# A new hand-written order for a grouped attention kernel, and VectorE's own addition of its terms in one more head

## The chip, the cores and the metric

The kernel runs on one core of one Trainium2 chip. The core has TensorE (matrix multiplication, called PE in the profile, its weight loads PEld), VectorE (DVE), ScalarE (ACT), GpSimd (POOL) and SyncE (SP), which work side by side and meet at semaphores. The metric is the device time of one execution in microseconds (us). Three timed executions and one profiled execution are at hand.

## The reference

```python
batch, n_q_heads, n_kv_heads, seq, head_dim = (8, 8, 2, 1024, 64)
scale = 1.0 / np.sqrt(head_dim)
for g in range(n_kv_heads):                      # four query heads share one k and v
    scores = scale * np.matmul(q_group, k_group.transpose(0, 1, 3, 2))
    scores_max = np.max(scores, axis=-1, keepdims=True)
    attn = np.exp(scores - scores_max)
    attn = attn / (np.sum(attn, axis=-1, keepdims=True) + 1e-08)
    output[:, q_start:q_end, :, :] = np.matmul(attn, v_group)
```

All arrays are float32. There are 64 attention problems (8 batches by 8 query heads), each 1024 by 1024 with 64 dimensions.

## The kernel before, in words

**The unit of work.** The 64 problems are called heads here and are numbered 0 to 63. The scores of a head are made transposed, keys on the partitions, in eight chunks. A chunk is made by two matmuls (line 791), each of 128 keys by 512 queries, one on the upper and one on the lower 64 rows of the array; they fill one of three PSUM slots, `sp0` to `sp2`, of 128 x 1024 float32 values. There are 512 chunks in all, here also called scores and counted from 0. A slot can be filled again only when the engine that reads it is done, so three chunks at most are on their way.

**Two engines take the exponential.** Of the 512 chunks, 377 go to ScalarE, which applies its exponential and writes the tile `pt` (line 801). The other 135 go to VectorE, which builds the exponential from the bits of a 16-bit number: `dpass` (line 813) reads PSUM and writes `yt`; then, for two chunks together where it can, `zh` (line 822) takes the mantissa into `zt`, `two` (line 830) takes the exponent into `et`, and `mul` (line 840) multiplies `zt` by `yt`. The exponential is the sum `et + zt`. In most heads nobody adds them: TensorE multiplies both with v and sums in PSUM, which costs it a second set of matmuls for such a chunk. In the last `TAIL` heads VectorE adds them itself (`add`, line 846), and TensorE has one set.

**GpSimd helps.** The planner hands some columns of a `mul` to GpSimd (line 775) wherever a free stretch of the shared work allows, but not in the last five heads (`GTO = 5`). GpSimd also issues the loads of q, k and v that change the type to bfloat16 (lines 560 and 550).

**The product with v.** For each of eight pieces of 128 queries in a head, eight matmuls (line 859) of 128 x 128 weights against 65 columns of `va` (v and a column of ones, which gives the row sums) are accumulated, plus one for each second term. The head before the last is stored through the same banks `ops0` and `ops1`, seven pieces at a time: `rec` (line 924) takes the reciprocals of the sums, `norm` (line 934) multiplies into `ost`, and SyncE stores a head when it is complete (line 943). The last head is accumulated chunk by chunk in a score slot (line 899) as its chunks come in. q and k are transposed on TensorE (line 569) and copied out by VectorE (lines 577 and 584).

**What sets the order.** Nothing is scheduled by the compiler. A long text, `ORDER`, is read letter by letter by the class `Plan`, which keeps one clock for each engine with costs in nanoseconds (the `M_` constants). For TensorE a letter is a score for ScalarE (`A`), a score for VectorE of the current head or of one of the next (`a`, `b`, `c`, `d`), three matmuls with v (`V`), a transposition (`T`), a warming matmul (`F`), a step of the first or last head (`E`, `L`), or a wait (`W`). For VectorE it is a `dpass` (`p`, `P`), a step of the chain in place 0, 1 or 2 of the list of open chains (digits), an eviction (`t`), `rec` (`r`, `R`), `norm` (`n`) or a wait (`i`). Which engine reads the next letter depends on whose clock is behind. The constants emit no instruction: they decide which engine a letter belongs to, how wide a part of a `mul` GpSimd is given, and when a load is due. The result is one list of instructions for each engine, in a fixed order. `W` and `i` leave nothing in the program; an engine waits where its next instruction's data or buffer isn't ready.

Of the kernel before, what the change touches and what calls it, by code (L numbers as in the profile page):

```python
# [18 lines left out]
M_SEE = 51  # L19
M_PAIR = 226  # L20
M_PTAIL = 205
M_SWITCH = 99
M_MM = 30.3
M_PVTAIL = 180
M_ACT = 917
M_ATAIL = 107
# [23 lines left out]
PB = 7  # L50
NPIECE = 8
GRAIN = 3
TAIL = 3
CHN = 2
LONG = 6
GFROM = 2
# [5 lines left out]


ORDER = """
ATAtWWWWWWWWWWWWWWWWWWWTAtFWEAbEpAEWWWWWaApEWEAFWW0WWWWbAEpWWAEWW0WWWTAtFFWW0WWWAbFFWWWWApEWWWWAR0cW
WWWAPWWWWWWWWWWWWAWWnWWWTRnVA0VVtVVVVA0WbWWWApVVVVVVVVVA0cWWWApVVVVVVVVA0WbWWWWApVVVVVVARWnWcVVVpVAV
VVA0WA0VVVT0VVtVVVVARnWbWVApVVVVVVA0VT0AVtVVVVA0cWWWApVVVVVVVVARnbWWWApVVVVVVVVA1cWWWApVVVVVVVVA00bW
WWWApVVVVVVVAR1bVVVPAVVVVVAnAV1VT0VVVVtVVARWWnWaAVpVVVVVVVAWW0WWWbApVVVVVVVVA0WbWWApVVVVVVVVVVARnAVT
1VVVVtVVVVA0WbWWApVVVVVVVVA0Vb0WAVpVVVVVVVVVAWRWW1WbAVPVVVVVVVVAWWnWWWbA0VVVVpVVVVVAVVV0VVVAAR1VTnVV
VVtVVAW1WWWbWApVVVVVVVVA0WbWWiWiWiWiWiAipVVVVVVVVAR1bWWWWAPVVVVVVVVAnbWW0WWAVpVVVVVVVA0WWWcWAVpVVVVV  # L70
VVARW0WAWVVT0VVVVtAVnVVVA0bWWWWWApVVVVVVVA1AVV0TVVVtVVVVA0bWWARPVVVVVVVVAnbViVipAVVVVA0WAR0VVVTnVVVt
VVVA0WWaWWApVVVVVVVVA0bVVpAVVVVVA0aVVApVVVVVVARnbVVpVAVVVVA1AVVTRnVVVVtVVA0WWWaWA0VVpVVVVVVVAW0WWWbA
VpVVVVVVVVARW1WbWWAVPVVVVVVVVAWnWWWbWA0VpVVVVVVVVVA0AVT1VVVtVVVVA1bWWWWARPVVVVVVVVAnWaVipVAVVVVA01Wb
VVVpVAVVVVVA0bWWWARVPVVVVVVVAnWWAWa1VVVVVpVVVAVVV0VVAAR0VTnVVVVtVVA0WWaWApVVVVVVVVA0WT0AVtVVVVARnaWW
WWApVVVVVVVVA0WaWWApVVVVVVVVVVVA0W0aWAVpVVVVVVVVVVVA0bWARVPVVVVVVVVVVAnAV1TVV0VVVVVtVAV0VVaARPVVVVVV
AVVnVaAipVVVVVAVVV1VAa1VVVVVpAVVVVVAR0naWWWApVVVVVVVVA1AVT0VVVVtVVVA0WaWWApVVVVVVVVARnaWWWWApVVVVVVV
VA0a0WWWAVpVVVVVVVVA0WWaWApVVVVVVVVVVARnbWWWApVVVVVVVAV0T0VAtVVVV0VaARVPVVAVVVVVnVAA0VVT0VVVtVVVA0aV
VpVAVVVVVARnaWWWApVVVVVVVVA0b0WWWAVpVVVVVVVAW0WWWaAVpVVVVVVVARWnWaWWApVVVVVVVVA0A0WWWaV0VVVVVpVVAVVV
VVRA0AVTnVVVtVVVA0WaVVpAVVVVVARnAVT0VVVVtVVA0WWWaWApVVVVVVVVA0aWWWApVVVVVVVVARnaWWWAVpVVVVVVVA1WWaWW
AVpVVVVVVVA0WWbWWApVVVVVVVVVARW0nWAVT1VVVVtVVVVA0AWWWa0VVVVVVVpVVVAVVVVA0aVRVPVVAVVVanAVpVVVAVVV0VVA  # L80
0bVApVVVVVVArnAVVT1VVtVVVVA0aWWWWApVVVVVVVVA0a0WWWAVpVVVVVVVARW1WaWWAVPVVVVVVVAnWWaWWA0VVpVVVVVVAVRV
1VAAnVVVT0VVtVVVVA0WaVVApVVVVVA0WWaWWWApVVVVVVVVAR1aWWWAPVVVVVVVVAnaWW0WAVpVVVVVVVVA1WbWAVpVVVVVVVVV
A0aWARVnVVVVVVpVVAVVVVVVRVAnT01AVtVVVVVV0AAV0TVVVtVVVVVA0aWWAipVVVVVVVVVaRnAWWWApVVVVVVVVVV0Ab0WWWWA
pVVVVVVVVARWnWaWWAVpVVVVVVVA0WWbWApVVVVVVAV0V0bAVpVVVVVVAV1VVARAnVVVT0VVVtVVVVVA0bWAVpVVVVVVVVARnAVV
T0VVtVVVA0WWaWWAVpVVVVVVVA0WWbWWAVpVVVVVVVA0WaWWARVPVVVVVVVAnVVVV1VAb0WWWApVVVVVVVVAR0WbWWWAVPVVVVVV
VAnWT1AVtVVVVA1bWWWWAipVVVVVVVVARnbWWWApVVVVVVVVA00AVT0VVVVtVVVARW0WbWWAVPVVVVVVVVAnbVipAVVVVVVV0Ab0
WWAVpVVVVVVVVAR0WbWWAVPVVVVVVAVnT1VAVtVVVVA1bWWARPVVVVVVVVAnbV0ipVAVVVVVV1AcV0VAVVVpVAVVVVVAR0bVVPAV
VVVVAnAV0VVT0VVVtVAV0VbARVPVVVVVVVAnWbWWAipVVVVVVVVVA0c0WWAVpVVVVVVVVARWW0WaWAVPVVVVVVVVAnWAWT1VVVtV
VVA1bVARPVVVVVVVAnbWWWA0pVVVVVVVVA1bWWWApVVVVVVVVAR1cWWWAPVVVVVVVVAnWAV0T1VVVtVVVA1WbWWWApVVVVVVVVV0
AcWAVRPVVVVVVVVVAnT1AVtVVVA1WbVVpAVVVVVVVRA0ncWWApVVVVVVVA1WAVVT1VVVtVVVVAR0bWWAVPVVVVVVVVVVAnWWcWAi  # L90
pVVVVVVVVVVA0AV0VVVVVVRV0bAVPVVVVVVVVAncWAipVVVVVVVVVV0AAR0VTnVVVVVtVAWW0WWWWbAVpVVVVVVA0WWWcWAVpVVV
VVVVARWW0WAVTnVVVtVVVA0WbWApVVVVVVVVA0WcWWWWWApVVVVVVVAR0AVVVnVVVVV0VbAipVVVVVAV0VVAcVpVVVVVAVVRVV0A
A0VVVVVnVVA0WbVVVVVVVVRAPVVVVVAnWWcWApVVVVVVVVA0A0VT0VVtVVVVVARnbWAVpVVVVVVVVA0AVVV0VVVVVV0VAbVVVpAV
VVVVA0VAAVVrVnVVVVVVVVVVRAnAVx0VVVV0VVV0VVVVVV0AAVVVVVVVRVnVVVAAVVVVVVVVVaApVVVVVVVVVVVranAApVVVVVVV
VVV0VVVa0AAVpVVVVVVVVVxVVRV0VVAAAVnVVVVVV0VVVVVVVVVVVVVVV0VVVVRV0VVVLnLLR0VVVVVVVVnVVVVVV0VVVVLLRnLL
LFFRFn
"""


# [29 lines left out]
class Plan:  # L129
# [121 lines left out]
    def dve(self, s):  # L251
# [26 lines left out]
        elif what in "pP":  # L278
            _, sl, j, c = s.dq.pop(0)
            n = len(STEPS) if j >= nj - TAIL else 3  # L280
            if s.open and s.open.nsteps != n:
# [74 lines left out]
    def turn(self, s, mode):  # L356
        if s.mode != mode:
            s.tP += M_SWITCH
            s.waste += M_SWITCH
            s.mode = mode  # L360

    def pe(self, s):
# [4 lines left out]
        if kind in "Aabcd":  # L367
# [12 lines left out]
            else:  # L380
                s.dcount[j] += 1
                if j == 0:
                    s.twice.append(c)
                if j < nj - TAIL:
                    s.mms[j] += 1
        elif kind == "V":
# [5 lines left out]
            s.ev.append((s.tP, "pv", s.pc, s.done, n))  # L392
            s.tP += n * M_MM
            s.done += n
# [9 lines left out]
        elif kind == "E":  # L404
# [5 lines left out]
            s.ev.append((s.tP, "pvf", c, s.fleft, None))  # L410
            s.tP += NPIECE * M_MM * (1 + (c in s.twice))
            if not s.fleft:
# [5 lines left out]
        elif kind == "L":  # L418
# [8 lines left out]
            s.ev.append((s.tP, "pvl", c, s.left, None))  # L427
            s.tP += NPIECE * M_MM
            if not s.left:
# [38 lines left out]
def kernel(  # L468
# [261 lines left out]
    def terms(j, par, only=range(NC)):  # L730

        for ci in only:
            c = ci if par == 0 else (ci + NH) % NC
            if (j, c) in where:
                ch, i = where[(j, c)]
                if j < NJ - TAIL:
                    yield ci, et[ch].bitcast(BF16)[:, i, par, :]
# [240 lines left out]
```

## Time and profile before

| what | us |
|---|---|
| median of three runs | 370.01 (369.92 to 370.11) |
| profiled execution, its own time | 369.21 |
| span of the profiled execution, first to last instruction | 367.3 |
| TensorE busy | 358.4 |
| VectorE busy | 353.4 |
| ScalarE busy | 353.3 |
| GpSimd busy | 258.5 |

The profiled execution is 0.80 us below the median of the timed runs, and 1.9 us of its time lie outside the span. A matmul counts as busy from its issue to its modelled end, and the next one starts long before that; a TensorE instruction that waits for a slot behind others does not show as idle. So the share of TensorE is read from the chain of waits and from the distance of its instructions, not from its busy time. VectorE instructions overlap as well: the next one begins some 0.08 us before the end of the one before it, where it does not depend on it.

### The profile page before, as it was taken

The page shows a single profiled execution, that of the slowest core. Times are in us where ns is not written, and L with a number is a line of the kernel's source. Part 1 is how long each engine was busy: PE and PEld are TensorE (multiplying, and loading weights), DVE is VectorE, ACT ScalarE, POOL GpSimd, SP SyncE. Part 2 cuts the span into 40 slices and gives each one's busy share as a digit, 9 for nine tenths or more (in the row PEclk, how much of TensorE's full clock was granted, in tenths as well). Part 3 has the DMA queues.
Part 4 walks back from the last instruction along what each step waited for, and adds up shares of the span by engine and source line. Part 5 has one row for each costly group of instructions (what it writes and reads, how often), then busy time and mean ns, then how long its engine had stood idle before and what let it go on. Part 6 is the DMA issues. An engine that isn't in the chain of part 4 may idle for free.

```text
span 367.3 us, 14608 instructions
## 1 busy us (share of the span) xinstructions
PE 358.4 (98%) x6498; PEld 239.0 (65%) x6498; DVE 353.4 (96%) x547; ACT 353.3 (96%) x381; POOL 258.5 (70%) x286
## 2 busy tenths in 40 slices
PE   8899999999999999999999999999999999999995
PEld 4466666666666765666666676766666667667675
DVE  4999999999999999999999999999999999999886
ACT  6999999999999999999999999999999999999981
POOL 5278878886899799894979878777787887520000
PEclk9999999999999999999999999999999999999999
DMA  7565156363257335255254426354353554112013
GB/s 146 101 113 113 62 104 117 48 141 82 68 102 112 106 89 102 59 110 129 72 100 87 104 75 141 66 98 109 90 86 85 129 116 75 60 46 89 32 59 145
DMA packets 39119, 34.62 MB, mean 94 GB/s; under 512 B 18192, under 2 KB 30608, under 8 KB 38928
## 3 DMA queue, kind: packets, MB, share of 16 engines
q0 software_dynamic: 10880, 12.19, 24.0%
q1 hardware_dynamic: 27888, 21.11, 18.5%
q8 instruction: 50, 0.82, 0.9%
q10 hardware_dynamic: 288, 0.39, 0.3%
q14 instruction: 13, 0.11, 0.1%
HBM read 27.13 MB, written 18.74 MB: 125 GB/s over the span
## 4 chain that ended last, share of the span: by engine, by line
PE 50%; DVE 41%; ACT 5%; issue 2%; DMA 1%; POOL 0%; DVEq 0%; POOLq 0%
PE ops L859 26%; PE sp L791 21%; DVE yt L813 20%; DVE et L830 5%; ACT pt L801 5%; DVE zt L822 5%; DVE ost L934 4%; DVE zt L840 3%; PE sp L569 3%; DVE qt L577 2%; DMA qs<-in_q_dram 1%; DVE rec L924 1%; DVE kt L584 1%; PE sp L899 1%; PE ops L879 0%
## 5 line engine op out<-in xcount | busy, mean ns | idle before, releaser
L801 ACT ACTIVATE pt<-sp 128x1024 bf16<-128x1024 f32 x377 | 350.8, 1033 | 2.9 <-PE sp L791 2.0
L775 POOL TENSOR_TENSOR zt<-yt,zt 128x560 bf16<-128x560 bf16 (+15 forms) x176 | 217.1, 1245 | 50.0 <-DVE zt L822 33.0
L859 PE MATMUL ops<-va,pt 128*128 128x65 bf16 x2904 | 179.4, 194 | 0.0
L791 PE MATMUL sp<-qt,kt 64*128 64x512 bf16 x1024 | 169.3, 382 | 3.2 <-ACT pt L801 0.9
L813 DVE TENSOR_SCALAR yt<-sp 128x1024 uint16<-128x1024 f32 x135 | 163.7, 1213 | 3.0 <-PE sp L791 2.5
L859 PEld LDWEIGHTS <-pt 128*128 128x128 bf16 x2904 | 138.6, 97 | 30.3 <-issue 30.3
L859 PE MATMUL ops<-va,zt 128*128 128x65 bf16 x1064 | 137.2, 194 | 0.0
L859 PE MATMUL ops<-va,et 128*128 128x65 bf16 x1024 | 131.7, 194 | 0.0
L859 PEld LDWEIGHTS <-et 128*128 128x128 bf16 x1024 | 87.1, 98 | 19.7 <-issue 19.7
L859 PEld LDWEIGHTS <-zt 128*128 128x128 bf16 x1064 | 90.9, 97 | 7.7 <-issue 7.7
L791 PEld LDWEIGHTS <-kt 64*128 64x128 bf16 x1024 | 49.7, 93 | 57.8 <-issue 33.6
L822 DVE TENSOR_SCALAR zt<-yt 128x2048 uint16<-128x2048 uint16 (+1 forms) x69 | 47.5, 688 | 0.6
L830 DVE TENSOR_SCALAR et<-yt 128x2048 uint16<-128x2048 uint16 (+1 forms) x69 | 47.1, 683 | 0.0
L934 DVE TENSOR_TENSOR ost<-ops,rec 128x448 f32<-128x448 f32 (+2 forms) x73 | 44.6, 611 | 1.1
L840 DVE TENSOR_TENSOR zt<-yt,zt 128x1144 bf16<-128x1144 bf16 (+36 forms) x63 | 38.3, 608 | 0.0
L560 POOL DMA_DIRECT2D qs<-in_q_dram x32 | 24.4, 763 | 9.4 <-PE sp L569 7.6
L577 DVE COPY qt<-sp 128x1024 bf16<-128x1024 bf16 (+1 forms) x32 | 21.5, 673 | 0.8 <-PE sp L569 0.8
L569 PE MATMUL sp<-ident,qs 128*128 128x128 bf16 x252 | 19.3, 219 | 0.3 <-DMA qs<-in_q_dram 0.2
L569 PEld LDWEIGHTS <-qs 128*128 128x128 bf16 x252 | 14.6, 98 | 1.6 <-issue 1.1
L924 DVE RECIPROCAL rec<-ops 128x7 f32<-128x7 f32 (+2 forms) x73 | 14.1, 193 | 0.9 <-PE ops L859 0.9
L770 POOL MEMSET tick<- 128x1 bf16 x55 | 11.4, 207 | 0.0
L560 POOL DMA_DIRECT2D ks<-in_k_dram x8 | 5.9, 737 | 5.9 <-PE sp L569 5.9
(44 smaller groups left out, 51.4 us busy)
## 6 DMA issues: line engine op xcount, KB each, us to landing
out_dram<-ost SPq DMA_DIRECT2D x63, 256.0 KB, 2.1
qs<-in_q_dram POOLq DMA_DIRECT2D x31, 256.0 KB, 4.2
kt<-kt SPq DMA_DIRECT2D x30, 64.0 KB, 2.5
va<-vd SPq DMA_DIRECT2D x30, 64.0 KB, 3.4
ks<-in_k_dram POOLq DMA_DIRECT2D x7, 256.0 KB, 4.5
vd<-in_v_dram POOLq DMA_DIRECT2D x7, 256.0 KB, 4.4
q<-in_q_dram ACTq DMA_DIRECT2D x1, 256.0 KB, 3.2
vs<-in_v_dram SPq DMA_DIRECT2D x1, 256.0 KB, 4.1
```

What stands on the lines that cost most here:

```text
L560: return nc.gpsimd.dma_start(out=t[:, 0:n, :], in_=x[lo : lo + n].rearrange("h (p s) d -> p h (s d)", p=128))
L569: nc.tensor.transpose(view[:, 0, c * 128 : (c + 1) * 128], src[:, c, :], ident)
L577: ins = nc.vector.tensor_copy(out=t[:, 0:n, :], in_=src)
L775: begun[j] = gps = nc.gpsimd.tensor_tensor(out=z, in0=flat(yt[j])[:, lo : lo + w], in1=z, op=ALU.mult)
L791: now = nc.tensor.matmul(sps[x][:, half, :], lhsT=t[lo : lo + D, c // NH, ci % NH * 128 : (ci % NH + 1) * 128], rhs=qt[j][lo : lo + D, 0, ...
L801: exps.append(nc.scalar.activation(out=p, in_=where_s[(j, c)], func=AF.Exp, scale=scale))
L813: vec = nc.vector.tensor_scalar(out=yt[ch][:, i, :, :], in0=where_s[c], scalar1=EXP_A, scalar2=EXP_B, op0=ALU.mult, op1=ALU.add,)
L822: vec = nc.vector.tensor_scalar(out=zt[j][:, 0:c], in0=yt[j][:, 0:c], scalar1=0x7F, scalar2=0x3F00, op0=ALU.bitwise_and, op1=ALU.bitwise_or,)
L830: vec = ins = nc.vector.tensor_scalar(out=et[j][:, 0:c], in0=yt[j][:, 0:c], scalar1=0x7F80, scalar2=None, op0=ALU.bitwise_and,)
L840: vec = nc.vector.tensor_tensor(out=z, in0=flat(yt[j])[:, 0 : cols[0]], in1=z, op=ALU.mult)
L859: ended[job] = nc.tensor.matmul(ops[plan.group_of[x] % 2][:, lo : lo + D + 1], lhsT=p[:, qs * 128 : (qs + 1) * 128], rhs=va[(b * G + h // ...
L934: vec = nc.vector.tensor_tensor(out=to, in0=src, in1=by, op=ALU.mult)
```

## The change

Two costs in the plan, the number of heads in which VectorE adds its terms, and the whole text `ORDER` are replaced. No function changes.

```diff
-M_SWITCH = 99
-M_MM = 30.3
+M_SWITCH = 96
+M_MM = 30.9
...
-TAIL = 3
+TAIL = 4
...
 ORDER = """
-ATAtWWWWWWWWWWWWWWWWWWWTAtFWEAbEpAEWWWWWaApEWEAFWW0WWWWbAEpWWAEWW0WWWTAtFFWW0WWWAbFFWWWWApEWWWWAR0cW
...
-LFFRFn
+ATAtWWWWWWWWWWWWWWWWWWWWTAtFFEAbEpEAWWWWWWAWWWWWWWWWWWaEpWWWEAFWWWWW0WWbAEpWAEFWW0WWTAtFFWW0WWWWAbF
...
+VVVRV0LLLLLnLLRLnVVVVVRVVnVVVVVVVVVVVVWWWWWWWWWWWWWWWWWWWWWWWWWWWWWWRWWWWWWWWWWWWWWWWWWWWWWWn
 """
```

`M_SWITCH` is what the plan charges TensorE for going from scores to other matmuls or back, and `M_MM` what it charges for one matmul with v. In what the two programs issue, the following differs; everything that is not named has the same number of instructions and the same sizes.

| engine | instructions | before | after |
|---|---|---|---|
| TensorE | matmuls with v | 5128 | 5120 |
| TensorE | changes between scores and other matmuls | 480 | 470 |
| VectorE | `zh`, and as many `two` | 69 | 68 |
| VectorE | `mul`: instructions, columns | 63, 56328 | 60, 60160 |
| VectorE | `add`: instructions, columns | 4, 6144 | 4, 7168 |
| GpSimd | parts of `mul`: instructions, columns | 176, 81912 | 173, 78080 |

VectorE takes 135 chunks in both, and ScalarE 377. Of the last four heads VectorE takes 2, 2, 3 and 1 chunks before, and 3, 1, 1 and 2 after. The end differs in form: before, the matmuls of the last head (line 899) stand on both sides of the last 48 of the head before it; after, all 64 of them stand ahead of those 48, so that the last `norm` and the last store are those of head 62 instead of those of head 63.

More of the change, by code (lines that the diff above doesn't have):

```diff
@@ L64 @@
 ORDER = """
-ATAtWWWWWWWWWWWWWWWWWWWTAtFWEAbEpAEWWWWWaApEWEAFWW0WWWWbAEpWWAEWW0WWWTAtFFWW0WWWAbFFWWWWApEWWWWAR0cW
[L66 to L94, printed above, removed]
@@ L95 @@
-VVV0VVVa0AAVpVVVVVVVVVxVVRV0VVAAAVnVVVVVV0VVVVVVVVVVVVVVV0VVVVRV0VVVLnLLR0VVVVVVVVnVVVVVV0VVVVLLRnLL
-LFFRFn
+ATAtWWWWWWWWWWWWWWWWWWWWTAtFFEAbEpEAWWWWWWAWWWWWWWWWWWWaEpWWWEAFWWWWW0WWbAEpWAEFWW0WWTAtFFWW0WWWWAbF
+FWWFFpAEA0TRAnWWWrWWtWWWWAWWWW0WWWbWWWAPVVVVVVVbnWWApVVVVVAVV0VA0cVVpVVVAVVVVRb0AWWWnWWWWWAVpVVVVVVA
+V0VT0AVtVVVVA0cWWWApVVVVVVVVARnbWWWApVVVVVVVVA1cWWWApVVVVVVVVA1cWWWWApVVVVVVVA2T0RVnAVVtVVVA0WWbWAVp
+VVVVVVVA0WWcWWApVVVVVVVVAR1bWWWAPVVVVVVVVAnbV0VpAVVVVVAR1TAnVVtVVVA0WbVVpVAVVVVVA0b0WWWWAVpVVVVVVVVA
@@ new lines @@
+RW1WAVTnVVVtVVVVA0WWbWWApVVVVVVVVVA0WbWWWWApVVVVVVVVVA0bWWW0WWAVVVpVVVVVVAVVRV0VAbnVVVVVpAVVVVVVA0AV
+VT0VVVtVVVVAR0WbWWWAVPVVVVVVVAnWbWWWAipVVVVVVVVA0a0WWWAVpVVVVVVVA0WWbWApVVVVVVVVARWnWbWWWApVVVVVVVVA
+1T1AVRVtVVVAnWbWWA0ipVVVVVVVVA0bWWWWApVVVVVVVARW0WAVTnVVVtVVVA0WbWWWApVVVVVVVVA1AVVT0VVVtVVVVVA0WaWW
+ApVVVVVVVVVARnbVVpVVAVVVVVA0b0WWWWAVpVVVVVVVA0WaWWApVVVVVVVVARnbWWWApVVVVVVVVA0a0WWWWApVVVVVVVVARnWA
+VT1VVVVtVVAW0WWWbAVpVVVVVVVA0Wa0WWAVVpVVVVVVAWWRWWW1WbAVPVVVVVVAVnVAb1VVVVpAVVVVVVVRAnAVT01VVVVVtVVV
@@ new lines @@
+A1WWbWApVVVVVVVVVA0WWbWWWApVVVVVVVVVVAR1bWWWAPVVVVVVVVAnbWWWA0VVVVpVVVAVVVV0AAVR1VVTnVVVVtVVAWW0WWWb
+AVpVVVVVAV0VVVaRnAVVVpVAVVVVVV0Aa0WWWAVpVVVVVVVAW0WWWbWAVpVVVVVVVARW1WaWWAVPVVVVVVVAnWbWWA0VpVVVVVVV
+ARW0WAVTnVVVtVVVA0WAVT0VVtVVVA0WWaWWWApVVVVVVVVA0bWWWWWAVpVVVVVVVVVARW0WAWVTnVVVtVVVA0WWaWWApVVVVVVV
+VVVA0bWWWApVVVVVVVVA0aWWWApVVVVVVVVARnbWWWWApVVVVVVVVA0bWWRWAPVVVVVVVVAnAV00VT0VVVVVtAVV0VAaVVpVVAVV
+VVAR0aVVPVVAVVVanAVpVVVVAVVV0bARVPVVAVVVVVnAA00VVVT0VVVtVVVA0WaWWAVVpVVVVVAVVrV0VAb0VVVAPVVVVVVAnWAV
@@ new lines @@
+0TVVVtVVVARnWaWWWAVpVVVVVAV0VbApVVVVVVVVA0WWaWWApVVVVVVVVVA1WAVVT0VVVVtVVVARWW0WbWWAVPVVVVVVVVAnWWWa
+WWAipVVVVVVVVA1AWWWbRV1VVVVVPVVAVVVAnaV0ipVVVAVVVV0VAAV0TVVrVtVVVA0WbVVPVAVVVVVAnaWiWiWiWiWiWiWiWiWi
+WiWiWiWiWiWiWiWiWiWiWiWiAipVVVVVVVVArnbWWWApVVVVVVVVA1bWWWA0pVVVVVVVVA0AV1TVV0VVVVAVtVVVVAr0aWWWAPVV
+VVVVVVAnaWiWiWiWiWiWiWiWiWiWiWiWiWiWiWiWiWiWiWiWiWiWiAipVVVVVVVVA1AWWWa1VVVV0VVVVApVVVVVARWnWbWWApVV
+VVVVVVA1WAVTr0VVVtVVVA0WWaWWAPVVVVVVVVAnbWWWRWAPVVVVVVVVAnAV0T0VVVVtVVVA0WWaAVpVVVVVVVVARnbWWAVpVVVV
@@ new lines @@
+VVVVA1aWWApVVVVVVVVVA00WbWWWWApVVVVVVVVARnAVVVT1VVVtVVVVVA1aWWAipVVVVVVVVVVV0bARnWAVVpVVVVVVVVVVA1bW
+WApVVVVVVVA0VTR0VAVtVVVAnbViVipVAVVVA0WAVVVT0VVtVVVVVA0aVRVPAVVVVAnWaViVipVAVVVVV0VA0aWWApVVVVVVVVA0
+aVVRVPAVVVVVAnAV1VVVVVb1WAVpVVVVVVVARWnWaWWAVpVVVVVVVA2WWbWAVpVVVVVVVAW2WWWbWApVVVVVVVVAR0nWAVT01VVV
+VtVVVA1WbAVpVVVVVVVVA0bWWWAVRPVVVVVVVVVAnWAT1VVVtVVVVA1bVVpVAVVVVVVVrAnbWWWA0ipVVVVVVVVVVA0AVT0VVVVt
+VVVVVA0bARVPVVVVVVVVVAnbWWiWiWiAipVVVVVVVVA0b0VVVApVVVVVVArW0WWbAVpVVVVVVVVAnAV0VT0VVVVVAtVVRVV0VAbn
@@ new lines @@
+WWWAVpVVVVVVVA0WbWWAVpVVVVVVVARW0WWbWAVPVVVVVVVAnWWbWA0VVVVpVVVVAVVVV0VA0aWWWApVVVVVVVVArnbWWWApVVVV
+VVVVA0T0AVtVVVA0aVrVPVVAVVVVb0AVPVVVAVVVVnAA0VVT0VVVtVVVVVAR0aWAPVVVVVVVVVAnbVipAVVVVVVV0AbR0WWAVVpV
+VVVVVVVAnWWAT0VVVtVVVA0WaVVpAVVVVVVA0AVVT0VVVRVVtVVVVAnaWAipVVVVVVVVVA0WaVVVVVpVAVVVVVAR0bWWAPVVVVVV
+VVVAna0WWAVVVpVVVVVVVVARW1WaAVpVVVVVVVVA0WanWWAVpVVVVVVVARWnWTA1VVVtVVVA0WaAVpVVVVVVVVA00aWWWApVVVVV
+VVVAR1AVTnVVVtVVVA0WaWWWApVVVVVVVVVVA0aWWAipVVVVVVVVVVAR0AVVnVVVVVV0VVVVA0AVV0VVVVVVaWARVPVVVVVVVVAn
@@ L97 @@
+AWaVVpVVVVVVVAW0WWWAWAV0VVVVVVV0VVVVVVVAARVnVVVVVVTVVtVVVVVVAaWWWWWWWWWWWWWWWWWApVVVVVVVVVARnaWWApVV
+VVVVVVA0aVVpVAVVVVVAR0aWWWAPVVVVVVVAnAV0VVVVVVVVVVA1AV0VVVVVVVVVVAR0AVVnVVVVV0VVVAAV0VVVVVVVVVVVArna
+VVVpVxVVAVVVVV0VARa0WWWWAPVVVVVVVVVVnVAa0AVVpVVVVVVVVVVVAR0WAWAVnVVVVVV0VVVVVVVV0VVVVVVV0VVVVVVVVVVV
+VVVRV0LLLLLnLLRLnVVVVVRVVnVVVVVVVVVVVWWWWWWWWWWWWWWWWWWWWWWWWWWWWWWWWWWWWRWWWWWWWWWWWWWWWWWWWWWWWn
 """
```

## The prediction

> **What bounds the kernel now.** I read the page's shares first, then the busy time by stretches, then the chain of waits of the last 50 us, then VectorE's own timeline there.
>
> ```profile
> span 367.3 us, 14608 instructions
> PE 358.4 (98%) x6498; PEld 239.0 (65%) x6498; DVE 353.4 (96%) x547; ACT 353.3 (96%) x381; POOL 258.5 (70%) x286
> 20.00:340.00 320.00, 317.77 (x5760) 211.34 (x5757) 318.15 (x484) 318.36 (x344) 250.01 (x270) 1.00 0.44 94
> 340.00:367.30 27.30, 23.32 (x566) 18.28 (x562) 20.89 (x37) 18.59 (x20) 0.00 (x0) 0.99 0.22 79
> L791 PE MATMUL sp<-qt,kt 64*128 64x512 bf16 x1024 | 169.3, 382 | 3.2 <-ACT pt L801 0.9 <-DVE yt L813 0.8 <-DVE qt L577 0.2
> ```
>
> The columns of the stretches are PE, PEld, DVE, ACT, POOL. From 20 to 340 us VectorE is busy for 318.15 of 320 us and ScalarE for 318.36: neither has 2 us left, and TensorE cannot be told from its 317.77. Its starts can. Where two chunks of scores follow each other, the second starts 0.22 us behind the first when a slot is free, but the mean over the 272 such places is 0.286: 17 us in which TensorE stands before a full slot. They end early:
>
> ```profile
> 321.81 1.00 PE sp L791 x6
> 322.82 0.84 PE ops L859 x24
> 323.66 0.56 PE sp L791 x4
> ...
> 344.59 0.54 PE sp L791 x4
> 345.13 1.54 PE ops L859 x47
> ...
> 359.70 0.75 PE sp L899 x24
> 360.45 1.46 PE ops L859 x48
> 361.91 1.26 PE sp L899 x40
> 363.17 0.02 issue
> 363.19 0.22 DVE rec L924
> ```
>
> In this chain two chunks take 0.54 (four matmuls), matmuls with v 0.031 each and changes included, and from 322 to 363.17 no piece of another engine stands between. So there are two regimes. Up to about score 464 (issued at 322.0) VectorE sets the pace, with ScalarE just behind it. From there TensorE does, and VectorE waits for it:
>
> ```profile
> 344.45 0.20 DVE L924 RECIPROCAL rec<-ops 128x7 f32<-128x7 f32 x1 [0.29 <-PE ops L859]
> 347.88 0.20 DVE L924 RECIPROCAL rec<-ops 128x7 f32<-128x7 f32 x1 [0.57 <-PE ops L859]
> 350.45 1.23 DVE L813 TENSOR_SCALAR yt<-sp 128x1024 uint16<-128x1024 f32 x1 [1.71 <-PE sp L791]
> 363.19 0.21 DVE L924 RECIPROCAL rec<-sp 128x8 f32<-128x8 f32 x1 [0.46 <-PE sp L899]
> ```
>
> That is 2.57 us of waiting between 344 and 350.45, where score 501 comes.
>
> **What the change costs, stage by stage.** Prices are distances between starts: VectorE's durations less the 0.08 us by which the next one overlaps.
>
> ```profile
> L813 DVE TENSOR_SCALAR yt<-sp 128x1024 uint16<-128x1024 f32 x135 | 163.7, 1213 | 3.0 <-PE sp L791 2.5 <-issue 0.2
> L830 DVE TENSOR_SCALAR et<-yt 128x2048 uint16<-128x2048 uint16 x66 | 45.9, 695 | 0.0
> L840 DVE TENSOR_TENSOR zt<-yt,zt 128x2048 bf16<-128x2048 bf16 x4 | 4.8, 1204 | 0.0
> L840 DVE TENSOR_TENSOR zt<-yt,zt 128x1024 bf16<-128x1024 bf16 x4 | 2.7, 670 | 0.0
> ```
>
> A column of `mul` is (1204 - 670)/1024 = 0.52 ns, and its fixed part 0.07 us after the overlap; `add` (1211 for 2048 columns, 686 for 1024) costs the same. `zh` and `two` of 2048 columns are 0.60, of 1024 columns 0.33. Where an instruction reads what the one just before it wrote, it starts 0.034 us after that one's end instead of 0.08 before: 0.116 lost. I counted the two programs' orders at these prices, cut at the chunks 460, 464 and 501.
>
> *VectorE ahead of its first chunk from 460 on.* `mul` goes from 55 instructions with 44,608 columns to 53 with 47,968 (+3360 x 0.52 - 2 x 0.07 = +1.6), because GpSimd is given 3,832 columns less over the whole kernel. One `two` of 2048 columns moves behind the cut (-0.6). Dependent neighbours fall from 41 to 36, mostly a `rec` with its `norm` right behind it (-0.6). Everything else is equal in number. Sum +0.4 us of 309, on the engine that sets the pace, so on the path.
>
> *VectorE between 460 and 501.* The `two` comes back, and with 1024 more columns of `add`, 472 more of `mul`, and one `mul` and one `zh` less, the sum is +1.2 us (0.5 + 0.5 + 0.24 - 0.14). The cover is the 2.57 us of waiting above: 1.4 remain. *From 501 on* the two orders hold the same instructions in another sequence: 13.2 us of work each, where the trace takes 13.74 (350.45 to 364.19).
>
> *TensorE.* Ahead of 464: 5 more matmuls with v (0.031 each), 4 fewer changes (0.095 each: 0.318 between the start of a score and of the following matmul with v, where the score itself takes 0.22), 4 more warming ones. Under 0.3 us, and covered by the 17 us before full slots. From 464 to 501: 4 fewer matmuls and 7 fewer changes, -0.12 - 0.66 = -0.8. Behind 501: 9 fewer matmuls and one change more, -0.2. Sum -1.0 us, on the path, since TensorE sets the pace there. VectorE follows: it needs 13.2 from chunk 501, and TensorE's 13.74 - 0.2 leave it 0.3.
>
> *ScalarE* has the same 377 exponentials, split alike at all cuts (336 ahead of 460, 368 ahead of 500).
>
> *The end.* Before, `rec` and two half `norm`s of head 63 and two stores of 128 KB follow the last matmul; after, `rec` (0.20), one `norm` of 384 columns (0.56) and one store of 256 KB. The instructions are 0.2 shorter (0.83 against 1.0); the landing of a 256 KB store is 2.1 in the median against 1.8 for the half one: together +0.1. The one `norm` of head 63, with `rec` and its store ahead on SyncE's queue, lies beside the last 48 matmuls (1.46 us) and costs nothing; without that cover it would cost its 0.9.
>
> *Moved loads.* GpSimd issues the same 40 casting loads and SyncE the same copies and stores, at other places in their queues. None ends a wait of TensorE above 0.5 us in the trace, so I put them at nothing. A load that came late would hold the transpositions behind it, then all scores.
>
> *What the counts do not hold: waits in the first stage.* Nothing in the trace shows how the new order meshes. VectorE loses 3.7 us between 20 and 340 in places other than dependent neighbours: 1.9 in `zh` and `two` that take up to 0.97 instead of 0.69 (15 of 132 are over 0.71), and 1.8 in waits, of which some could go with TensorE's true distance in the plan (0.031, near the new constant, against 0.0303). Lower bound: the 1.8 vanish. Upper bound: the 3.7 come once more. I take 0: the mesh is already within 1% of full, and a new one of the same kind is nearest to the old.
>
> **Two rules weighed.** The row above gives TensorE's weight loads 65% of the span. The Trainium skill (Perfetto Trace Analysis, Identifying the Most-Contended Engine) would judge TensorE by that figure, not by the 98% of its matmuls, and name the engine with the highest occupancy as the one to improve: VectorE with 96%. By the rule alone TensorE's -1.0 is worth nothing and VectorE's +1.6 counts whole. That speaks against the change and gives 371.6. The chain shows it right up to 322 us and wrong behind it, so I count +0.4 and -1.0.
>
> The second concerns the stretched `two`. One began at 54.68 and took 0.91, with GpSimd's load issue from 54.33 to 55.09 beside it. The skill (SBUF — State Buffer, the port table's practical consequences) says that the later of the two "fully blocks" until the other has finished. Taken so, this one would have begun work 0.41 late; it ended 0.22 late. At the trace's price a collision costs some 0.13 (1.9 over 15), at the rule's up to three times that. The number of issues stays at 40, so I leave the sum as it is, and the upper bound above takes in a doubling.
>
> **The sum.** +0.4 - 1.0 + 0.1 = -0.5 us, so 368.7 against the profiled execution's 369.21; the median of the runs is 0.8 above that: 369.5.
>
> **Rivals.**
>
> - *VectorE's extra work reaches the end* (slower). If its chunk 501 is ready in the slot before VectorE has come to it, the 2.57 us are gone and the tail is VectorE's: then the +1.2 counts as well, and the -1.0 does not: +0.4 + 1.2 + 0.1 = +1.7, 371.7. For it: two `add`s and three whole `mul`s now stand close together ahead of that chunk. Against it: 1.4 us of cover should be left. It decides when the waits ahead of that chunk fall under 1.2.
> - *The first stage meshes better* (faster). The 1.8 us of VectorE's waits shrink by a half to the whole: -0.5 - 1.2 = -1.7, 368.3. For it: the plan's distance for the 5,120 matmuls is now the measured one. Against it: TensorE had 17 us of slack there, so its price was hardly what cost VectorE time.
> - *The first stage meshes worse* (slower). The same 1.9 to 3.7 us come on top: about +2, 372.
> - *The constants do nothing.* They emit nothing, and if TensorE is never late where they count, only the order's counts remain: that is my forecast, not another number.
>
> **How the numbers follow.** Some 0.2% (0.74 us) is what a measurement of this kernel can tell from no change. Forecast with its own spread, 368.9 to 370.3: 0.5, of which 0.12 falls below 369.27. Better mesh: 0.18, all faster. VectorE's tail: 0.17, worse mesh: 0.15, nearly all slower (0.02 of it within). So faster 0.30, within 0.2% 0.40, slower 0.30. The range of 368.2 to 371.7 leaves out about the best tenth and the worst tenth.
>
> **What would show it.** Right: VectorE busy up by about 1.5 us in all; in the chain TensorE alone from about 320 us to the end; VectorE's wait for the score near 350 shrunk from 1.71 to about 0.5 to 1 but not gone; the last matmul near 362.6. Wrong: a chain of the last 20 us with VectorE in it (first rival); busy VectorE in 20 to 340 under 317 of 320, or `zh` and `two` with means above 0.72 (worse mesh); ScalarE's last exponential before 358 (better mesh).

## The result and the profile after

The changed kernel takes 374.9 us in the median of four runs (374.29 to 377.7), the kernel before 370.06 in the runs beside it. The ratio is 1.0136, with a 95% interval of 1.0108 to 1.0165. That is slower, where the forecast was 369.5 with a range up to 371.7. The profiled execution has a time of 374.29 and a span of 372.5 us, 5.2 more than before.

The page of the changed kernel, shares and costliest groups (its line numbers are one higher than before):

```profile
span 372.5 us, 14579 instructions
PE 360.2 (97%) x6491; PEld 240.3 (65%) x6491; DVE 358.1 (96%) x542; ACT 354.1 (95%) x381; POOL 249.0 (67%) x282
L802 ACT ACTIVATE pt<-sp 128x1024 bf16<-128x1024 f32 x377 | 351.5, 1033 | 6.6 <-PE sp L792 5.3
L792 PE MATMUL sp<-qt,kt 64*128 64x512 bf16 x1024 | 170.9, 383 | 5.8 <-DVE yt L814 4.0
L831 DVE TENSOR_SCALAR et<-yt 128x2048 uint16<-128x2048 uint16 (+1 forms) x68 | 50.0, 735 | 0.0
```

Three things differ at once: ScalarE is idle for 6.6 us instead of 2.9, TensorE's scores wait for VectorE's reads of PSUM for 4.0 instead of 0.8, and the step `two` (line 831) costs 735 ns on average instead of 683 (47.1 us in 69). GpSimd does less. Two of these groups in the kernel before:

```profile
L801 ACT ACTIVATE pt<-sp 128x1024 bf16<-128x1024 f32 x377 | 350.8, 1033 | 2.9 <-PE sp L791 2.0
L830 DVE TENSOR_SCALAR et<-yt 128x2048 uint16<-128x2048 uint16 (+1 forms) x69 | 47.1, 683 | 0.0
```

The stretches of the changed kernel's trace (columns PE, PEld, DVE, ACT, POOL, then the granted clock) say where:

```profile
0.00:20.00 20.00, 17.43 (x185) 9.23 (x186) 13.98 (x27) 16.46 (x19) 8.09 (x18) 1.00 0.68 131
20.00:40.00 20.00, 16.67 (x270) 10.49 (x266) 18.82 (x23) 15.56 (x18) 13.80 (x13) 0.91 0.32 62
60.00:80.00 20.00, 19.83 (x361) 13.18 (x360) 19.97 (x30) 20.00 (x23) 17.57 (x21) 1.00 0.53 87
```

Between 20 and 40 us ScalarE finishes 18 exponentials instead of the 23 of a full stretch. The timelines of VectorE and GpSimd there, and the longest waits of that stretch:

```profile
18.31 0.66 DVE L578 COPY qt<-sp 128x1024 bf16<-128x1024 bf16 x1
18.89 3.94 DVE L831 TENSOR_SCALAR et<-yt 128x2048 uint16<-128x2048 uint16 x1
22.75 1.21 DVE L814 TENSOR_SCALAR yt<-sp 128x1024 uint16<-128x1024 f32 x1
```

```profile
17.84 0.33 POOL L776 TENSOR_TENSOR zt<-yt,zt 128x80 bf16<-128x80 bf16 x1 [1.91 <-DVE rec L925]
18.30 0.59 POOL L551 DMA_DIRECT2D vd<-in_v_dram  x1
18.92 3.35 POOL L776 TENSOR_TENSOR zt<-yt,zt 128x280 bf16<-128x280 bf16 x3
22.21 0.78 POOL L561 DMA_DIRECT2D qs<-in_q_dram  x1
```

```profile
ACT pt L802 <- PE sp L792: 4.2, 2, 3.3
PE sp L792 <- DVE yt L814: 3.2, 1, 3.2
DVE yt L814 <- PE sp L792: 0.6, 1, 0.6
DVE rec L925 <- PE ops L860: 0.5, 1, 0.5
```

One `two` of 2048 columns takes 3.94 us instead of 0.68. Beside it GpSimd runs three parts of a `mul` without a gap (280, 848 and 392 columns by the order of instructions), from 18.92 to 22.27. VectorE reads no PSUM meanwhile, TensorE stands for 3.2 us before a full slot, and ScalarE for 3.3 without a score. TensorE comes back at 24.0 with its full clock and loses half of it 1.2 us later (the same columns as above):

```profile
24.00:25.18 1.18, 1.17 (x19) 0.70 (x18) 1.18 (x2) 0.74 (x1) 0.00 (x0) 1.00 0.67 109
25.18:28.60 3.42, 3.42 (x39) 1.92 (x38) 2.37 (x4) 2.43 (x4) 1.02 (x1) 0.50 0.73 153
28.60:30.00 1.40, 1.40 (x23) 0.73 (x21) 1.34 (x4) 1.29 (x2) 1.05 (x2) 1.00 0.04 5
```

The granted clock is 0.50 from 25.18 to 28.60 us; matmuls with v start 0.05 to 0.06 us apart there instead of 0.031, and VectorE, which had nothing to wait for at 23, now waits 0.6 and 0.5 us for TensorE. From score 20 to score 40 the changed kernel needs 17.7 us (19.31 to 37.03 in TensorE's timeline), the kernel before 14.3. The difference is not made good later.

Why three parts in a row? VectorE's steps `zh`, `two` and `mul` and GpSimd's instructions take turns at what the source calls the port; what is seen of it here is that the two engines wait for each other. The order of GpSimd is fixed. In the changed order a load of v for the second key group (`cv`, line 551) stands just ahead of the three parts. It is added to the list after the plan has been made, so the plan's clock of GpSimd does not contain it. Its issue takes 0.59 us, and the part of 280 columns, which should have been through by then, begins when VectorE's step begins. Each part has a hold, a wait put in by hand, on the VectorE instruction *ahead* of the step it must not disturb (`gate` in the source); for the parts of 848 and 392 columns that is the copy that ended at 18.97. The plan trusts that VectorE, already in place, takes the port first. GpSimd now had it first, the hold of the next two parts was already met, and they followed without giving it back. (By its recorded start the step is a little ahead of the part, 18.89 against 18.92, but it overlaps the copy, which ends at 18.97. That VectorE can't take the port before that end is a reading; no run shows it.) In the kernel before, the same load had one part behind it, and VectorE's step began before that part:

```profile
19.05 0.59 POOL L550 DMA_DIRECT2D vd<-in_v_dram  x1
19.67 1.03 POOL L775 TENSOR_TENSOR zt<-yt,zt 128x280 bf16<-128x280 bf16 x1
```

```profile
19.39 0.75 DVE L830 TENSOR_SCALAR et<-yt 128x2048 uint16<-128x2048 uint16 x1
```

### The profile page after: what moved, and what is told of

It reads as the page before. It is cut to its first block, busy times and chain, and to the rows that moved or that the text cites. A ratio compares the mean times of both kernels' runs of the same rounds, so it can differ in the third digit from the quotient of the medians.

```text
span 372.5 us, 14579 instructions
## 1 busy us (share of the span) xinstructions
PE 360.2 (97%) x6491; PEld 240.3 (65%) x6491; DVE 358.1 (96%) x542; ACT 354.1 (95%) x381; POOL 249.0 (67%) x282
## 4 chain that ended last, share of the span: by engine, by line
PE 74%; DVE 21%; issue 1%; DMA 1%; ACT 1%; POOL 0%; POOLq 0%
PE ops L860 37%; PE sp L792 32%; DVE yt L814 11%; PE sp L570 4%; DVE et L831 3%; DVE zt L841 2%; DVE ost L935 2%; DVE zt L823 2%; DMA qs<-in_q_dram 1%; DVE qt L578 1%; ACT pt L802 1%; PE sp L900 1%; DVE rec L925 0%; PE ops L880 0%; DVE kt L585 0%
## 5 line engine op out<-in xcount | busy, mean ns | idle before, releaser
L776 POOL TENSOR_TENSOR zt<-yt,zt 128x560 bf16<-128x560 bf16 (+18 forms) x173 | 207.4, 1211 | 56.4 <-DVE zt L823 37.9
L860 PEld LDWEIGHTS <-pt 128*128 128x128 bf16 x2912 | 140.7, 98 | 30.2 <-issue 30.2
L860 PE MATMUL ops<-va,et 128*128 128x65 bf16 x1016 | 129.8, 194 | 0.0
L860 PEld LDWEIGHTS <-zt 128*128 128x128 bf16 x1056 | 91.9, 97 | 8.0 <-issue 7.8
L792 PEld LDWEIGHTS <-kt 64*128 64x128 bf16 x1024 | 50.9, 93 | 63.2 <-issue 39.2
L831 DVE TENSOR_SCALAR et<-yt 128x2048 uint16<-128x2048 uint16 (+1 forms) x68 | 50.0, 735 | 0.0
L823 DVE TENSOR_SCALAR zt<-yt 128x2048 uint16<-128x2048 uint16 (+1 forms) x68 | 47.1, 692 | 0.6
L841 DVE TENSOR_TENSOR zt<-yt,zt 128x2048 bf16<-128x2048 bf16 (+40 forms) x60 | 40.1, 669 | 0.0
L570 PE MATMUL sp<-ident,qs 128*128 128x128 bf16 x252 | 19.3, 219 | 0.5 <-DMA qs<-in_q_dram 0.3
L925 DVE RECIPROCAL rec<-ops 128x7 f32<-128x7 f32 (+2 forms) x73 | 14.3, 195 | 0.8 <-PE ops L860 0.8
```

Of the source, the lines that this page charges most:

```text
L570: nc.tensor.transpose(view[:, 0, c * 128 : (c + 1) * 128], src[:, c, :], ident)
L776: begun[j] = gps = nc.gpsimd.tensor_tensor(out=z, in0=flat(yt[j])[:, lo : lo + w], in1=z, op=ALU.mult)
L792: now = nc.tensor.matmul(sps[x][:, half, :], lhsT=t[lo : lo + D, c // NH, ci % NH * 128 : (ci % NH + 1) * 128], rhs=qt[j][lo : lo + D, 0, ...
L823: vec = nc.vector.tensor_scalar(out=zt[j][:, 0:c], in0=yt[j][:, 0:c], scalar1=0x7F, scalar2=0x3F00, op0=ALU.bitwise_and, op1=ALU.bitwise_or,)
L831: vec = ins = nc.vector.tensor_scalar(out=et[j][:, 0:c], in0=yt[j][:, 0:c], scalar1=0x7F80, scalar2=None, op0=ALU.bitwise_and,)
L841: vec = nc.vector.tensor_tensor(out=z, in0=flat(yt[j])[:, 0 : cols[0]], in1=z, op=ALU.mult)
```

## The experiments

The kernels ran in two groups, each on one chip together with the kernel before, whose median was 370.31 us in the first (experiments 1 to 4) and 370.00 in the second (5 to 7). The changed kernel as it stands was not run again; it is compared by its ratio to the kernel before, 1.0136. Theory: the load makes GpSimd late, and parts that nothing holds pile up on the port. Rivals: the new order as such; the load's issue itself; the addition in the fourth head from the end.

**1. The load earlier, in the changed kernel.** The planned place of the load moves from 18.0 to 15.8 us (16.0 in the expectations is this edit).

```diff
-    ev.append((max(at - 16000, 18000), "cv", None, (b, g), None))
+    ev.append((max(at - 16000, 15800), "cv", None, (b, g), None))
```

> The changed kernel with one edit: the first load of v for the second group, which is not in the plan, is placed at 16.0 us instead of 18.0, ahead of GpSimd's part of 80 columns and in a stretch in which GpSimd waits. Theory (the load's issue makes GpSimd late, its three parts of 280, 848 and 392 columns then run back to back and hold the port for the whole 3.3 us that VectorE's step at 18.9 us needs): that step takes about 0.7 us instead of 3.94, the wait of TensorE and its low clock around 27 us go with it, and the time falls by 4 to 5 us, to about 370 to 371. Rival (the new order as such leaves too little room near the start, whatever the load does): still 373 or more, with VectorE's waits elsewhere before 40 us.

Measured: 370.71 us in the median of 12 runs, ratio to the kernel before 1.0015 (0.9995 to 1.0035). The step and GpSimd beside it:

```profile
19.46 0.68 DVE L831 TENSOR_SCALAR et<-yt 128x2048 uint16<-128x2048 uint16 x1
20.06 1.22 DVE L814 TENSOR_SCALAR yt<-sp 128x1024 uint16<-128x1024 f32 x1
```

```profile
16.49 0.54 POOL L551 DMA_DIRECT2D vd<-in_v_dram  x1
18.41 1.00 POOL L776 TENSOR_TENSOR zt<-yt,zt 128x80 bf16<-128x80 bf16 x2 [1.38 <-DVE rec L925]
19.62 3.05 POOL L776 TENSOR_TENSOR zt<-yt,zt 128x848 bf16<-128x848 bf16 x2 [0.20 <-DVE qt L578]
```

GpSimd does the same work: the 280 columns are through before 19.46, VectorE takes the port, and the 848 wait for it. The changed kernel was 4.84 us above the kernel before, this one is 0.40 above it: the move of one load by 2 us returns 4.4 us, nearly the whole loss.

**2. A strict hold for every part.** Each part of GpSimd waits for the end of VectorE's last step on the port, not for the instruction ahead of it.

```diff
-            tc.add_manual_dep(gps.ins, gate.ins.name, Sync, reason="the port goes to the step behind it")
+            tc.add_manual_dep(gps.ins, port.ins.name, Sync, reason="the port step is over")
```

(`port` is set to the step itself where `gate` was set to the one ahead.)

> The changed kernel with one edit: each of GpSimd's parts waits for the end of VectorE's last step that uses the shared port, instead of for the instruction ahead of that step. Theory (parts that come late overtake the step because nothing holds them): only the part of 280 columns can still stand before the step at 18.9 us, which then takes about 1.4 us instead of 3.94; steps stretched to 0.9 us become rare; 371 to 372.5. Rival (the stretch comes from the load's issue itself or from the amount of work on GpSimd): the step stays near 4 us, the time within 0.5 us of 374.5.

Measured: 377.57 us, ratio 1.0191 (1.0174 to 1.0207), slower than the changed kernel. The step of the stall did shrink, to 1.32 us, but VectorE's steps as a whole grew. Its groups by form, in this kernel first and then in that of experiment 1:

```profile
L830 DVE TENSOR_SCALAR et<-yt 128x2048 uint16<-128x2048 uint16 x67 | 48.5, 723 | 0.0
L822 DVE TENSOR_SCALAR zt<-yt 128x2048 uint16<-128x2048 uint16 x67 | 48.2, 719 | 0.6
```

```profile
L823 DVE TENSOR_SCALAR zt<-yt 128x2048 uint16<-128x2048 uint16 x67 | 46.9, 700 | 0.6
L831 DVE TENSOR_SCALAR et<-yt 128x2048 uint16<-128x2048 uint16 x67 | 46.4, 692 | 0.0
```

In VectorE's timeline 39 of these steps take over 0.71 us instead of 11, and 32 `mul`s are longer than their columns explain, instead of none; together these steps and `mul`s take 7.2 us more than in experiment 1. The reading is that parts that start later end later, in the next step. The half of my expectation that spoke of the one step held, the other (371 to 372.5, fewer stretched steps) did not: the early hold is worth more than it costs.

**3. No parts in the chain of the stall.** A chain is the steps from `zh` to `mul` for two chunks; the stretched `two` belongs to chain 1 (`j == 1`). VectorE does its 2048 columns alone; the load stays where it was.

```diff
+        elif kind == "gmul" and j == 1:
+            pass
...
+            if j == 1:
+                cols = [2048]
```

> The changed kernel with one edit: in the one chain of the stall VectorE does all 2048 columns of the product, GpSimd none (its four parts are left out), and the load stays where it was. Theory (the parts hold the port): the step takes 0.7 us, VectorE pays 1600 columns, about 0.8 us, more, and the time is 370.5 to 371.5. Rival (the issue of the load alone blocks VectorE): the step stays over 2 us and the time over 373.

Measured: 371.1 us in 20 runs, ratio 1.0021 (1.0011 to 1.0031). VectorE's step takes 0.68 us, though the issue of the load ends right at its beginning as in the changed kernel, and another load follows it there:

```profile
20.87 0.53 POOL L551 DMA_DIRECT2D vd<-in_v_dram  x1 [2.28 <-PE sp L794]
```

```profile
21.45 0.68 DVE L833 TENSOR_SCALAR et<-yt 128x2048 uint16<-128x2048 uint16 x1
```

Its end at 21.40 lies 0.05 us ahead of the step. The load alone does not stall VectorE; the parts behind it do.

**4. The same fault put into the kernel before.** The load moves to 23.0 us, ahead of four parts.

```diff
-    ev.append((max(at - 16000, 18000), "cv", None, (b, g), None))
+    ev.append((max(at - 16000, 23000), "cv", None, (b, g), None))
```

> The kernel before with one edit: the same load at 23.0 us instead of 18.0, so that it is issued just ahead of four parts of GpSimd (448, 560, 240, 504 columns) and makes the first of them about 0.6 us late. Theory: the first part then runs into VectorE's step at 24.25 us, the other three are no longer held by anything, and all four pass; that step takes about 3.5 to 4 us instead of 0.68, and the kernel before becomes slower by 3 to 5.5 us, 373 to 375.5. Rival (the stall belongs to the new order): within 0.7 us of 370.

Measured: 376.08 us, ratio 1.0176 (1.0125 to 1.0226), a loss like that of the changed kernel and somewhat above what I had expected (373 to 375.5).

```profile
23.95 0.53 POOL L550 DMA_DIRECT2D vd<-in_v_dram  x1 [2.22 <-PE sp L791]
24.50 3.92 POOL L775 TENSOR_TENSOR zt<-yt,zt 128x448 bf16<-128x448 bf16 x4
```

```profile
24.57 4.40 DVE L830 TENSOR_SCALAR et<-yt 128x2048 uint16<-128x2048 uint16 x1
```

The first part begins 0.07 us ahead of the step, and all four pass. The old order has the same weakness; it had not met it.

**5. A strict hold in the one chain.** As in experiment 2, but only for the parts of the chain of the stall, with the load where it was.

```diff
+            gate_now = port if j == 1 else gate
+            tc.add_manual_dep(gps.ins, gate_now.ins.name, Sync, reason="the port goes to the step behind it")
```

> The changed kernel with the load where it was, and one edit: in the chain of the stall alone, GpSimd's parts wait for the end of VectorE's step that they overtook, instead of for the instruction ahead of it. Theory (the missing hold lets 848 and 392 columns pass): only the part of 280 stays ahead of the step, which takes 1.3 to 1.5 us instead of 3.94; 371 to 372. Rival (the late part of 280 columns with the load is what costs, the other two matter little): over 373.

Measured: 371.08 us in 14 runs, ratio 1.003 (1.0016 to 1.0044).

```profile
19.12 1.32 DVE L833 TENSOR_SCALAR et<-yt 128x2048 uint16<-128x2048 uint16 x1
```

```profile
19.16 0.73 POOL L776 TENSOR_TENSOR zt<-yt,zt 128x280 bf16<-128x280 bf16 x1
20.53 2.68 POOL L776 TENSOR_TENSOR zt<-yt,zt 128x848 bf16<-128x848 bf16 x2 [0.64 <-DVE et L833]
```

The late part of 280 columns costs 0.64 us (1.32 - 0.68); what made 3.26 of it were the two parts behind, which nothing held back.

**6. The load earlier, in the kernel before.** The edit of experiment 1.

> The kernel before with the load at 16.0 us instead of 18.0. In the kernel before the load's issue runs into a step at 19.39 us that it lengthens by less than 0.1 us. Theory (the load costs only where parts pile up behind it): within 0.3 us of the kernel before. Rival (the early load is a gain of its own, which the first experiment then owes to it): 0.5 us or more faster.

Measured: 370.19 us in 14 runs, ratio 1.0001 (0.9986 to 1.0017). The early load is no gain of its own.

**7. The addition undone.** Experiment 1's kernel, with head 60 as before: VectorE adds 3072 columns less, TensorE issues 24 matmuls more.

```diff
-                if j < NJ - TAIL:
+                if j < NJ - 3:
...
+            own = [i for i in range(c) if jobs[j][i] >= NJ - 3]
...
+            if job == NJ - 4 and stop == NC:
+                stop = len(every)
```

> The changed kernel with the load at 16.0 us (as in the first experiment), and the other part of the change undone: VectorE no longer adds the terms of head 60 (3072 columns, about 1.6 us, less), TensorE multiplies both terms with v instead (24 matmuls, 0.75 us, more). Theory (in the last 40 us TensorE sets the pace and VectorE has no more than a few tenths to spare): 0.3 to 0.8 us slower than with the addition, 371 to 371.5. Rival (the addition made VectorE the bound of the tail): 0.5 to 1 us faster, 369.7 to 370.2.

Measured: 371.65 us, ratio to the kernel before 1.0045 (1.0028 to 1.0063), against 1.0015 (0.9995 to 1.0035) with the addition. From score 464 to the end of the last matmul its trace has 41.33 us, that of experiment 1 has 40.68: 0.65 more, where 24 matmuls are 0.75. So the second part of the change was a small gain in the trace, as TensorE's pace in the tail had suggested. The medians agree with its sign, but the two intervals overlap.

None of these kernels is faster than the kernel before.

## Why the prediction was wrong, step by step

**The step that failed** is "Moved loads": GpSimd's 40 loads "at other places in their queues", put at nothing because none ended a wait of TensorE's. I asked what waits for the data of a load. The cost came from what stands *behind* it on GpSimd. By the change, two more parts of one `mul` came to stand behind the load, ahead of a VectorE step with a hold that does not hold. Experiments 1, 3, 4 and 5 show it from four sides; in the trace it is worth 17.7 - 13.2 = 4.5 us between scores 20 and 40 (13.24 in experiment 1), in the medians, each against the kernel before beside it, 4.4.

**The second rule weighed** was misread in the trace before. The Trainium skill (SBUF — State Buffer, practical consequences of the port table) says that of a VectorE step in its fast mode and a GpSimd instruction the later "fully blocks". I priced a collision at 0.13 us by the mean of 15 stretched steps, set that against the rule, and thought a doubling of the total the worst. But the 15 speak for the rule: 14 of them end 0.49 or 0.50 us after the issue of a load ends, the fifteenth 0.55 after a part ends, however long the overlap was. A step of 0.68 us that is blocked until just before that end would do this. So 0.13 was the mean of short overlaps, not a softer block. The stall fits too: 18.89 + 3.94 = 22.83 is GpSimd's end at 22.27 and some 0.6 us, the step's own length. What neither the rule nor my bound had is that GpSimd's next part takes the port again before VectorE gets it, so the price is that of the queue, not of one instruction. The bound of 3.7 us for the first stage was close to the size; I gave it 0.15 and put it down to "mesh".

**The sum without the stall** can be read in experiment 1, since it holds everything else of the change. Times between TensorE's starts and ends:

| step | forecast | kernel before | experiment 1 | measured |
|---|---|---|---|---|
| first stage, score 20 to 464 | +0.4 | 302.76 | 303.48 | +0.7 |
| tail, score 464 to the end of the last matmul | -1.0 | 41.12 | 40.68 | -0.4 |
| last matmul to the end of the span | +0.1 | 4.17 | 4.49 | +0.3 |

So the counted -0.5 was +0.6 in the trace, and +0.4 in the medians (370.71 against 370.31), within what the measurement can tell from nothing. (The table begins at score 20, which is issued at 19.27 us before and 19.89 in experiment 1; that start scatters from 19.3 to 22.0 over all traces.) The three signs were right. The first stage fits its reason: VectorE's busy time in it grew by 0.9 us, from 301.07 to 301.95, where I had counted 0.4.

The tail was mis-sized. The changed kernel has the same 40.68, so the size is not chance. In its two pieces, 464 to 501 and from there on (first before, then changed):

```profile
322.03:349.94 27.91, 27.91 (x568) 19.47 (x566) 25.56 (x40) 27.91 (x32) 2.05 (x2) 1.00 0.18 60
349.94:363.15 13.21, 13.21 (x350) 11.20 (x347) 12.19 (x21) 8.65 (x10) 0.00 (x0) 1.00 0.25 92
```

```profile
327.20:354.51 27.31, 27.30 (x564) 19.57 (x563) 25.80 (x37) 27.31 (x31) 1.63 (x1) 1.00 0.18 56
354.51:367.88 13.37, 13.32 (x337) 10.85 (x333) 13.03 (x24) 9.16 (x10) 0.00 (x0) 1.00 0.23 87
```

The first piece gained 0.6 instead of 0.8; the second lost 0.15 where I had a gain of 0.2. What the forecast left out is ScalarE, the fourth number: in the first piece it shows no idle time in either kernel (27.91 of 27.91, 27.31 of 27.31). I had found its exponentials equal in number and put nothing down for it. The chain that shows TensorE alone does not show the short waits of a score before a full slot. The longest of them:

```profile
356.52 0.54 PE sp L792 x4
357.06 0.04 issue
357.10 0.39 PE sp L792 x2
```

```profile
355.91 1.14 ACT L802 ACTIVATE pt<-sp 128x1024 bf16<-128x1024 f32 x1
```

The third of these scores begins behind the end of an exponential, at 355.91 + 1.14 = 357.05, and waits for the semaphore that ScalarE raises. An estimate from the starts of all scores of the tail (what lies beyond 0.22 us behind a score and 0.10 behind a matmul with v, from 0.04 on) puts such waits at 0.4 us before and 0.85 in the changed kernel; 0.3 and 0.6 of these end with an exponential, the rest with a read by VectorE. The increase, 0.4, is most of the missing 0.6: with less work TensorE came up against ScalarE, and to a smaller part against VectorE. This is read from the traces; no experiment takes it apart.

The end of the span scatters by more than the forecast term: 4.2 to 5.4 us in the three traces with the old end, 4.2 to 5.0 in the six with the new one. One sum is misprinted: the parenthesis of VectorE's sum between 460 and 501 adds up to 1.1, while the instructions that it counts give the stated 1.2.

**The two regimes** and the first rule weighed (TensorE's load share of 65% as the measure) came out as told in one respect: in the tail 24 matmuls more cost 0.65 us (experiment 7), although VectorE's busy time there fell by 1.3 (38.84 to 37.56). That TensorE alone is at its limit there was too simple, as read above.

**The rivals.** "Worse mesh" named a time nearer to the truth, 372, without the mechanism. Of the signs that I had set for it, two came: VectorE was busy for 316.55 of the 320 us, under 317, and the mean of `two` went over 0.72 (0.735; that of `zh` stayed at 0.692). But one step alone did the latter, with 3.26 of the 3.5 us; a mean was the wrong instrument.

Of "VectorE's extra work reaches the end", the cover came out as forecast: VectorE's waits ahead of chunk 501 were to shrink from 2.57 us to 1.4, and are 0.24 (at 334.41) + 0.51 + 0.59 = 1.34. But they lie earlier than I had them, and the chunk itself (at 355.14) is no longer waited for, where I had said 0.5 to 1:

```profile
339.38 0.69 DVE L578 COPY qt<-sp 128x1024 bf16<-128x1024 bf16 x1 [0.51 <-PE sp L570]
340.66 1.23 DVE L814 TENSOR_SCALAR yt<-sp 128x1024 uint16<-128x1024 f32 x1 [0.59 <-PE sp L792]
...
355.14 1.21 DVE L814 TENSOR_SCALAR yt<-sp 128x1024 uint16<-128x1024 f32 x1
```

That rival would have made the tail 1.2 us longer; it became 0.4 shorter.

## What to carry to other kernels

When an order changes, look along every in-order queue for an instruction that the plan's clock does not contain, and ask what stands behind it and whether each of those is held by something that is still in the future when it runs late. A hold on the instruction ahead of a step works only while both engines are on time; it is cheap and right on average, and it fails whole. Search a trace for single instructions several times their median before reading any mean.

## What the runs showed of the hardware that I had not expected

GpSimd's instructions kept the port from VectorE across instruction boundaries: three parts in a row held a 0.68 us step for 3.26 us, four for 3.72 (4.40 in all). Load issues were not seen to do this: two of the 15 stretched steps before had a second issue right behind the first, and ended 0.49 and 0.50 us after the first. A stall of TensorE of 3.2 us was followed, 1.2 us after its end, by 3.4 us at a granted clock of 0.50, with another 1.1 us of waiting for VectorE at 26 to 29 us. That is no chance of one execution: the mean granted clock was 0.992 or less in all four executions of the changed kernel, and 0.997 or more in ten of the twelve of experiment 1, where the stall is gone. The Trainium skill (TensorE: Matmul & The Clock Gate, The HAM clock gate) describes such a halving after an idle stretch of about 3.4 us; the stretch here was 3.2 us as the waits give it. And a hold that is later by one VectorE step, applied everywhere, cost 7 us (377.57 against 370.71 in experiment 1), more than the stall that it shortens.
